# An eighth home for W1 tiles, and a later block 1 whose x is transposed by DMA alone, in the early phase of a two-layer MLP kernel

## The chip, the cores and the metric

The kernel runs on one core of one Trainium2 chip. The time is the device time of one execution in microseconds (us), lower is better. Most executions of one kernel agree within 0.3%.

## The reference

```
x: 16 x 512 x 768, w1: 768 x 3072, b1: 3072, w2: 3072 x 768, all float32
y = x @ w1 + b1
y = 0.5 * y * (1 + erf(y / sqrt(2)))      # gelu
out = y @ w2
```

## The kernel before

The 8192 rows of x are worked off in eight blocks of 1024 rows. Both products use a scheme of the Strassen kind: seven products P1 to P7 of half-size operands in place of eight, at the price of sums of operands (on VectorE, DVE) and of results (DVE and ScalarE, ACT). A *unit* of the first product is one tile of 256 columns of W1 with one block of x. A unit takes seven groups of three matmuls of 512 columns, 4.53 us when nothing waits.

A *W1 tile* in SBUF has seven operands: four raw quarters and three sums that DVE makes (one raw quarter is also replaced by a difference). There are twelve tiles. The first 20 us or so are the *head*: loads, casts, and the first two tiles with block 0 by plain products. In the early phase (blocks 0 and 1) each tile is loaded from W1 by GpSimd's queue (it casts to float16), completed by DVE, used by block 0 and by block 1, and stored once, 672 KB, by SyncE's queue into a scratch in DRAM (`keep`), from where blocks 2 to 7 read it. There are seven *homes* for twelve tiles, so tiles 7 to 11 take over the homes of tiles 0 to 4 when block 1 has used those. The rows of W2 are loaded into the last homes as they come free.

In the code and the profiles, `bX`, `bY`, `bZ` and `bW` are the buffers in PSUM into which TensorE writes the products, `arena` is the memory in SBUF that holds everything else, and c12 and c22 are two of the four quarters of a unit's result. A *slot* is a place between the products of a unit where work for the other engines and queues is emitted. A hole is time in which PE has no matmul to execute.

The order of units and of the loads and stores around them (cut):

```
slots.update({7: slots[0], 8: slots[1], 9: slots[2], 10: slots[3], 11: slots[4]})   # homes of tiles 7 to 11

seq = ([(0, k) for k in range(7)] +                                  # (block, tile)
       [(1, 0), (1, 1), (1, 2), (0, 7), (1, 3), (0, 8), (1, 4), (0, 9), (1, 6), (0, 10), (0, 11),
        (1, 5), (1, 10), (1, 11), (1, 7), (1, 8), (1, 9)])
over = {7: 0, 8: 1, 9: 2, 10: 3, 11: 4}

def loads_a(pos):                      # GpSimd's queue, emitted at slot 5 of unit `pos`
    if pos == 0:
        load_wt(4); load_next_x(1, (0, 4, 1, 5)); load_wt(5)
        load_next_x(1, (2, 6, 3, 7)); load_wt(6)
    for n in range(7, NH):
        if pos == at[1, over[n]] + 1:  # one unit after block 1 used the old tile of that home
            load_wt(n)
    if pos in w2_at_pos:
        load_w2(*w2_at_pos[pos])

X1_PE = (3, 7)                         # x tiles of block 1 that TensorE transposes
def transposes_a(pos):                 # SyncE's queue
    for t in (pos - 1, pos + 3):
        if t not in X1_PE:
            transpose_dma(1, t)

# ... in fill_a(pos, slot), at slot 5:
loads_a(pos)
if pos < 5:
    transposes_a(pos)
for n in {at[1, 0]: (0, 2, 3, 4, 6, 5), at[1, 1]: (1,)}.get(pos, ...):
    keep(n)                            # SyncE's queue too
```

The pipeline of one unit i and of the unit j before it, where the waits below arise (cut): 

```
p1(i); copy_xy(i)   # ACT copies bX into bY once P1 is done
p7(j)               # then DVE adds c22 from bY
fill(1)
p5(i); p3(j)        # then DVE adds c12 from bZ
p6(i)               # into bY; then DVE copies bY into bZ
j.right_done()      # ACT: gelu of c12 and c22
p4(j)               # then ACT: gelu; p2(i), then ACT: gelu
```

Every engine executes its own instructions in this order.

Of the kernel before, what the change touches and what calls it, by code (L numbers as in the profile page):

```python
# [10 lines left out]
P = 128  # L11
ADD = mybir.AluOpType.add
SUB = mybir.AluOpType.subtract
# [4 lines left out]
B11, B21, T1, B22, T3, T2, T4 = range(7)  # L18
# [4 lines left out]
def kernel(  # L23
# [8 lines left out]
    nc = tc.nc  # L32
# [5 lines left out]
    RH = SB // 2  # L38
    nsb = R // SB
    KQ = K // P // 2  # L40
    NH = H // P // 2
# [26 lines left out]
    GR = 4 * NH * RH  # L68
# [20 lines left out]
    def cut(off, n, pattern=None, **dims):  # L89
        ap = arena[:, off:off + n]  # L90
        return ap.rearrange(pattern, **dims) if pattern else ap

    def halves(off):
        return [cut(off + h * (GR // 2), GR // 2, "p (c a r) -> p c a r", c=NH, a=2)
                for h in range(2)]

    Gs = [halves(0), halves(GR)]
# [17 lines left out]
    def wt_at(off):  # L115
        return cut(off, WT_N)

    def w1_raw(wt):
        return wt[:, 0:4 * KQ * P].rearrange("p (k c) -> p k c", c=2 * P)
# [9 lines left out]
    W2P = 2 * W2_N  # L129
    o_far = [o_w2 + W2P, o_w2 + W2P + WT_N, o_w2 + W2P + 2 * WT_N, o_w2 + W2P - WT_N]  # L130
    slots = dict(enumerate([wt_at(o_wt + k * WT_N) for k in range(3)] + [wt_at(o) for o in o_far]))
    slots.update({7: slots[0], 8: slots[1], 9: slots[2], 10: slots[3], 11: slots[4]})
    wt_late = [wt_at(o_wt2), wt_at(o_wt2 + WT_N)] + wt_own[:2]
    wt_far = [wt_at(o_lev + 8 * RH + k * WT_N) for k in range(3)]
    assert 8 * RH + 3 * WT_N <= 8 * LB
# [20 lines left out]
    w2rows = [cut(o_w2 + k * W2P, W2P, "p (c n) -> p c n", c=NH) for k in range(2)]  # L156
# [29 lines left out]
    with tc.manual_schedule():  # L186

        soon, queue, late, slow = [], [], [], []

        def tt(o, a, b, op):  # L190
            nc.vector.tensor_tensor(out=o, in0=a, in1=b, op=op)  # L191

        def later(n, f, q=None):
            (queue if q is None else q).append((70 + n * 0.52, f))
# [8 lines left out]
        def flush(q):  # L203
            while q:
                q.pop(0)[1]()
# [4 lines left out]
        def hi_of(n):  # L210
            sb, k = divmod(n, NH)
            return k if sb < ONE else k // 2 + NQ * (k % 2)

        def load_wt(n):
            hi = hi_of(n)
            if n >= NH:
                sb, k = divmod(n, NH)
                wts[n] = wt_far[k - 4] if 4 <= k < 7 else wt_late[(sb + 2 + k - 7 * (k > 6)) % 4]
                nc.sync.dma_start(out=wts[n], in_=w1s[hi][:])
                return  # L220
            wts[n] = slots[n]
            nc.gpsimd.dma_start(out=w1_raw(wts[n]), in_=w1r[:, :, 2 * hi * P:2 * (hi + 1) * P])

        def keep(n):
            nc.sync.dma_start(out=w1s[hi_of(n)][:], in_=wts[n])

        def prep_wt(n):
            o = {s: w1_op(wts[n], s) for s in range(7)}
            for d, a, b in ((T3, B22, T1), (T1, T1, B11), (T2, B22, T1), (T4, B21, T2)):
                later(KQ * P, lambda d=d, a=a, b=b: tt(o[d], o[a], o[b], SUB), soon)  # L230

        def load_w2(k, c0, c1):
            nc.gpsimd.dma_start(out=w2rows[k][:, c0:c1, :], in_=w2r[:, k, c0:c1, :])
# [65 lines left out]
        def xT_of(sb, t):  # L299
            return XTs[sb][:, t // NU, :, (t % NU) * P:(t % NU + 1) * P]  # L300

        def transpose_dma(sb, t):
            nc.sync.dma_start_transpose(out=xT_of(sb, t), in_=xhs[t])
# [5 lines left out]
        def transpose_pe(sb, t, copy=nc.scalar.copy):  # L309
            for kc in range(2 * KQ):  # L310
                nc.tensor.transpose(out=bT[t % 2][:, kc, :], in_=xhs[t][:, kc * P:(kc + 1) * P],
                                    identity=ident[:])
            copy(out=xT_of(sb, t), in_=bT[t % 2][:])
# [5 lines left out]
        def x_sums(sb, q, r=slice(0, RH), ks=range(4)):  # L319
            A11, A12, A21, A22 = [a[:, :, r] for a in blocks(sb)]  # L320
            S1, S2, S4 = [a[:, :, r] for a in XSs[sb]]
            n = KQ * len(range(RH)[r])
            ops = ((S1, A21, A22, ADD), (S2, S1, A11, SUB), (A21, A11, A21, SUB), (S4, A12, S2, SUB))
            for k in ks:
                later(n, lambda k=k: tt(*ops[k]), q)
# [431 lines left out]
        def plain(n, row, side, half, r=slice(0, RH)):  # L757
            slot = ((B11, T1), (B21, B22))[half][side]
            for c in range(KQ):
                nc.tensor.matmul(out=banks[n, row][side][:, r], lhsT=w1_op(wts[n], slot)[:, c, :],  # L760
                                 rhs=blocks(0)[2 * row + half][:, c, r],
                                 start=half == 0 and c == 0 and r.start == 0,
                                 stop=half == 1 and c == KQ - 1, skip_group_check=True)

        def plain_done(n, row, side):
            nc.scalar.activation(out=Gs[0][side][:, n, row, :], in_=banks[n, row][side][:, 0:RH],
                                 func=GELU, bias=b1t[:, 2 * n + side:2 * n + side + 1])

        top, bottom = slice(0, 2 * P), slice(2 * P, RH)
        for half in range(2):  # L770
            for side in range(2):
                plain(0, 0, side, half)
        for side in range(2):
            plain_done(0, 0, side)
        plain(1, 0, 0, 0)
        transpose_pe(0, 4)
        plain(1, 0, 0, 1)
# [27 lines left out]
        for k in (2, 3):  # L805
            for r in (top, bottom):
# [2 lines left out]
        soon += last  # L809


        seq = ([(0, k) for k in range(7)] +
               [(1, 0), (1, 1), (1, 2), (0, 7), (1, 3), (0, 8), (1, 4), (0, 9), (1, 6), (0, 10), (0, 11),
                (1, 5), (1, 10), (1, 11), (1, 7), (1, 8), (1, 9)])
        at = {u: n for n, u in enumerate(seq)}
        over = {7: 0, 8: 1, 9: 2, 10: 3, 11: 4}

        def load_next_x(sb, ts):
            for t in ts:
# [1 line left out]

        w2_at_pos = {8: (0, 0, 2), 9: (0, 2, 4), 11: (0, 4, 6), 13: (0, 6, 8),
                     at[1, 6] + 1: (0, 8, 10), at[1, 6] + 2: (0, 10, 12),
                     at[1, 5] + 1: (1, 7, 12), at[1, 10] + 1: (1, 0, 3), at[1, 11] + 1: (1, 3, 7)}

        def loads_a(pos):
            if pos == 0:
                load_wt(4)
                load_next_x(1, (0, 4, 1, 5))
                load_wt(5)  # L830
                load_next_x(1, (2, 6, 3, 7))
                load_wt(6)
            for n in range(7, NH):
                if pos == at[1, over[n]] + 1:
                    load_wt(n)
            if pos in w2_at_pos:
                load_w2(*w2_at_pos[pos])

        X1_PE = (3, 7)

        def transposes_a(pos):
            for t in (pos - 1, pos + 3):
                if t not in X1_PE:
                    transpose_dma(1, t)

        def fill_a(pos, slot):
            if pos == 2 and slot == 1:
                plain(1, 1, 1, 1, bottom)
                plain_done(1, 1, 1)
            if pos == at[1, 0] - 2 and slot in (2, 5):  # L850
                transpose_pe(1, X1_PE[slot // 3])
            if slot == (1 if pos < at[1, 0] else 4) and pos + 1 < len(seq) and seq[pos + 1][0] == 0:
                prep_wt(seq[pos + 1][1])
            if slot == 4:
                if pos in (3, 6):
                    prep_wt(pos // 6)
                for m, c in ((21, 9), (22, 0), (23, 3), (23, 6)):
                    if pos == m:
                        prep_w2(T2, c, queue)
                        prep_w2(T3, c, late if m == 23 else queue)  # L860
                if pos == 23:
                    for c in range(0, NH, W2C):
                        prep_w2(T4, c, late)
            if slot == 1:
                if pos in (at[1, 0] - 2, at[1, 0] - 1):
                    h = pos - at[1, 0] + 2
                    x_sums(1, soon, slice(h * RH // 2, (h + 1) * RH // 2))
                if pos == at[0, NH - 1] + 2:
                    for c in range(0, NH, W2C):
                        prep_w2(T1, c, queue)  # L870
                    for k in (0, 1):
                        g_sum(k, 0)
            if pos > at[0, NH - 1]:
                if slot in (1, 4):
                    sums((0, 1100, 0, 0, 1500)[slot])
            elif slot in (1, 2, 4, 5):
                sums((0, 600, 300, 0, 600, 300)[slot])
            if slot == 5:
                loads_a(pos)
                if pos < 5:  # L880
                    transposes_a(pos)
                for n in {at[1, 0]: (0, 2, 3, 4, 6, 5), at[1, 1]: (1,)}.get(
                        pos, seq[pos][1:] if pos > at[1, 6] and seq[pos][0] and seq[pos][1] > 6 else ()):
                    keep(n)
            if slot == 6:
                flush(soon)

# [230 lines left out]
```

## Time and profile before

| | before |
|---|---|
| time, median (three runs) | 853.24 us |
| span of the profiled run | 851.5 us |
| TensorE (PE) busy | 844.9 us, 99% |
| DVE busy | 667.0 us, 78% |

The page of the profile of the kernel before: the span, the busy time of PE with its share and count of instructions, and the chain of work that ended last, by engine (PEld is TensorE's weight load, POOL is GpSimd).

```profile
span 851.5 us, 16488 instructions
PE 844.9 (99%) x6432; PEld 568.8 (67%) x6432; DVE 667.0 (78%) x1128; ACT 420.9 (49%) x686; POOL 83.3 (10%) x135
...
PE 94%; DMA 4%; DVE 1%; ACT 0%; issue 0%; POOL 0%; DVEq 0%; ACTq 0%
```

PE is the limit, so only holes in its stream of matmuls, or work that it need not do, can be won. I find holes by subtracting the start of each matmul from that of the next: 512 columns take 216 ns when nothing waits. The timeline of the kernel before (start, duration, engine, line, operation, output and input, count, and in brackets the idle time before it with what ended it) shows what the early phase holds of both kinds:

```profile
35.44 0.50 PE L311 MATMUL bT<-ident,arena 128*128 128x128 f16 x6
36.37 0.81 ACT L313 COPY arena<-bT 128x768 f16<-128x768 f16 x1
...
37.72 0.50 PE L311 MATMUL bT<-ident,arena 128*128 128x128 f16 x6
...
41.63 1.46 PE L386 MATMUL bY<-arena 128*128 128x512 f16 x6 [0.17 <-ACT bY L604]
...
46.46 0.68 DVE L611 TENSOR_TENSOR arena<-bY,arena 128x512 f32<-128x512 f32 x1
```

The two lines with bT are the PE transposes of two x tiles (they shift the stream by 0.33 us each). At 41.63 us PE waited for ACT's copy into bY (matmul 0.335 us late). The DVE add at 46.46 us released a matmul 0.31 us late; a further hole of 0.08 us is at 45.95 us. Together that is 1.39 us, all that the early phase has to give.

First SyncE's in the timeline: six transposes, issued from 23.35 us on, take it 14.45 us, and then seven stores follow.

```profile
23.35 14.45 SPq L303 DMA_TRANSPOSE arena<-arena  x6
37.89 8.99 SPq L225 DMA_DIRECT2D w1s<-arena  x7
```

GpSimd's load of the first tile that reuses a home (tile 7), in the timeline:

```profile
51.54 0.83 POOL L222 DMA_DIRECT2D arena<-in_w_dram  x1 [26.17 <-PE bZ L386]
```

### The profile page before, as it was taken

Reading aid. Unit: us, or ns where it says so; the run is one execution under the profiler, and the core shown is the slowest. Engines: PE = TensorE matmul, PEld = TensorE weight load, DVE = VectorE, ACT = ScalarE, POOL = GpSimd, SP = SyncE. Lnnn points to the kernel's source line nnn. Section 1 sums busy time; section 2 is a strip of 40 time slices with the busy share of each in tenths; the row PEclk is TensorE's granted clock in tenths of the full one; section 3 lists DMA queues with packets and bytes.
Section 4 is the critical chain, followed back from the end, with each engine's and each line's share of the span. In section 5 each row is a group of like instructions: output and inputs, shape, how many; then the busy total and the mean of one; then the engine's idle time right before and its main releaser. Section 6 shows DMA issues by size and latency. Waiting matters only on the chain.

```text
span 851.5 us, 16488 instructions
## 1 busy us (share of the span) xinstructions
PE 844.9 (99%) x6432; PEld 568.8 (67%) x6432; DVE 667.0 (78%) x1128; ACT 420.9 (49%) x686; POOL 83.3 (10%) x135
## 2 busy tenths in 40 slices
PE   8999999999999999999999999999999999999998
PEld 5444445687544897448974499645995469944798
DVE  4866678786657998579976799668996689956998
ACT  4777762122277512784138722477216771267611
POOL 5021100002100002000020000200002100010000
PEclk9999999999999999999999999999999999999999
DMA  9996986749999599987999689994999969984398
GB/s 227 213 256 89 253 169 244 267 184 221 212 340 226 186 326 372 304 183 233 334 368 292 141 283 335 360 294 113 312 335 355 277 128 325 347 322 172 100 298 295
DMA packets 143522, 219.05 MB, mean 257 GB/s; under 512 B 61756, under 2 KB 84724, under 8 KB 143444
## 3 DMA queue, kind: packets, MB, share of 16 engines
q1 hardware_dynamic: 117968, 179.83, 66.8%
q0 software_dynamic: 25440, 38.15, 20.7%
q8 instruction: 50, 0.82, 0.4%
q14 instruction: 28, 0.23, 0.1%
q10 hardware_dynamic: 36, 0.01, 0.0%
HBM read 180.30 MB, written 47.87 MB: 268 GB/s over the span
## 4 chain that ended last, share of the span: by engine, by line
PE 94%; DMA 4%; DVE 1%; ACT 0%; issue 0%; POOL 0%; DVEq 0%; ACTq 0%
PE bY L386 20%; PE bY L491 15%; PE bX L386 13%; PE bX L491 10%; PE bW L386 7%; PE bZ L386 7%; PE bZ L491 5%; PE bW L491 5%; PE bY L430 5%; DMA arena<-in_x_dram 3%; PE bZ L430 2%; PE bX L430 2%; PE bW L430 2%; DMA arena<-in_w_dram 1%; PE bY L578 1%; DVE arena L191 1%
## 5 line engine op out<-in xcount | busy, mean ns | idle before, releaser
L191 DVE TENSOR_TENSOR arena<-arena 128x1536 f16<-128x1536 f16 (+7 forms) x632 | 402.9, 668 | 7.8 <-DMA arena<-arena 1.6
L386 PEld LDWEIGHTS <-arena 128*128 128x128 f16 x1974 | 192.5, 98 | 224.7 <-issue 1.1
L491 PEld LDWEIGHTS <-arena 128*128 128x128 f16 x3528 | 292.1, 98 | 8.3 <-issue 0.4
L386 PE MATMUL bY<-arena 128*128 128x512 f16 x846 | 214.5, 379 | 0.3 <-ACT bY L604 0.2
L611 DVE TENSOR_TENSOR arena<-bY,arena 128x512 f32<-128x512 f32 (+1 forms) x102 | 69.3, 680 | 126.3 <-PE bY L386 87.6
L491 PE MATMUL bY<-arena 128*128 128x192 f16 x1500 | 138.3, 246 | 0.0
L386 PE MATMUL bX<-arena 128*128 128x512 f16 x564 | 138.2, 379 | 0.0
L604 ACT COPY bY<-bX 128x512 f32<-128x512 f32 (+1 forms) x143 | 78.6, 550 | 119.3 <-DVE arena L540 81.9
L402 ACT ACTIVATE arena<-arena,b1t 128x1024 f16<-128x1024 f32 x94 | 108.0, 1149 | 54.4 <-DVE arena L639 54.4
L624 ACT COPY arena<-bW 128x512 f32<-128x512 f32 (+1 forms) x147 | 81.0, 551 | 91.0 <-PE bW L491 43.9
L491 PE MATMUL bX<-arena 128*128 128x192 f16 x1020 | 93.1, 246 | 0.1
L639 DVE TENSOR_TENSOR arena<-bZ,arena 128x512 f32<-128x512 f32 (+1 forms) x102 | 69.2, 679 | 20.7 <-PE bZ L386 17.9
L386 PE MATMUL bZ<-arena 128*128 128x512 f16 x282 | 76.2, 379 | 0.0
L386 PE MATMUL bW<-arena 128*128 128x512 f16 x282 | 76.2, 379 | 0.0
L430 PEld LDWEIGHTS <-arena 128*128 128x128 f16 x528 | 51.6, 98 | 34.1 <-issue 0.2
L523 POOL DMA_DIRECT2D out_dram<-arena x42 | 30.5, 728 | 404.8 <-DVE arena L635 368.2
L407 ACT ACTIVATE arena<-bX,b1t 128x512 f16<-128x512 f32 x94 | 64.0, 681 | 10.0 <-PE bX L386 10.0
L407 ACT ACTIVATE arena<-bY,b1t 128x512 f16<-128x512 f32 x94 | 63.3, 673 | 0.0
L655 ACT COPY bZ<-bY 128x512 f32<-128x512 f32 (+1 forms) x54 | 29.0, 537 | 65.9 <-DVE arena L639 33.7
L297 POOL DMA_DIRECT2D arena<-in_x_dram x60 | 32.3, 544 | 250.8 <-DMA arena<-arena 141.3
L491 PE MATMUL bZ<-arena 128*128 128x192 f16 x504 | 48.5, 246 | 0.0
L491 PE MATMUL bW<-arena 128*128 128x192 f16 x504 | 48.5, 246 | 0.0
(60 smaller groups left out, 398.9 us busy)
## 6 DMA issues: line engine op xcount, KB each, us to landing
arena<-w2s SPq DMA_DIRECT2D x294, 288.0 KB, 4.6
arena<-w1s SPq DMA_DIRECT2D x72, 672.0 KB, 7.1
out_dram<-arena POOLq DMA_DIRECT2D x42, 384.0 KB, 7.2
w2s<-arena SPq DMA_DIRECT2D x49, 288.0 KB, 3.7
arena<-in_x_dram POOLq DMA_DIRECT2D x60, 192.0 KB, 7.3
w1s<-arena SPq DMA_DIRECT2D x12, 672.0 KB, 6.6
arena<-in_w_dram POOLq DMA_DIRECT2D x17, 384.0 KB, 7.4
out_dram<-arena SPq DMA_DIRECT2D x17, 384.0 KB, 3.3
```

Source lines behind the costliest of these rows:

```text
L191: nc.vector.tensor_tensor(out=o, in0=a, in1=b, op=op)
L297: nc.gpsimd.dma_start(out=xhs[t], in_=xr[:, sb * 8 + t, :])
L386: nc.tensor.matmul(out=dst[:, 0:RH], lhsT=w1_op(self.wt, slot)[:, c, :], rhs=a[:, c, :], start=first and c == 0, stop=c == self.C - 1, ski ...
L402: nc.scalar.activation(out=self.G[1][:, hi, :, :], in_=self.tmp, func=GELU, bias=b1t[:, 2 * hi + 1:2 * hi + 2])
L407: nc.scalar.activation(out=self.G[0][:, hi, row, :], in_=bank[:, 0:RH], func=GELU, bias=b1t[:, 2 * hi:2 * hi + 1])
L430: nc.tensor.matmul(out=dst[:, 0:N2], lhsT=a, rhs=w[:, :, c, :], start=first and c == 0, stop=c == self.C - 1, skip_group_check=True)
L491: nc.tensor.matmul(out=dst[:, t * N4:(t + 1) * N4], lhsT=a, rhs=w[:, c, :], start=first and c == 0 and t == ts[0], stop=c == NQ - 1, skip_ ...
L523: eng.dma_start(out=orr[:, s0:s0 + 2, right * N2:(right + 1) * N2], in_=self.dst[:, r].rearrange("p t h n -> p t (h n)"))
L604: nc.scalar.copy(out=bY[u.g % 2][:, 0:u.F], in_=bX[u.g % 2][:, 0:u.F])
L611: nc.vector.tensor_tensor(out=u.c22(), in0=bY[u.g % 2][:, 0:u.F], in1=w[:, 0:u.F], op=ADD)
L624: nc.scalar.copy(out=w[:, 0:u.F], in_=bW[:, 0:u.F])
L639: nc.vector.tensor_tensor(out=u.c12(), in0=bZ[:, 0:u.F], in1=w[:, 0:u.F], op=ADD)
```

## The change

The intent: take the two PE transposes off TensorE by giving them to the DMA engines; to give these time, begin block 1 one unit later, which takes one more tile of W1 and so an eighth home (in a part of block 1's output that is written late); and relieve DVE at 38 to 47 us by making six sums of tiles 0 and 1 in the head, where DVE idles, and by spreading the sums of block 1's x. The first load of W2 rows, which would otherwise be free to start at once, is held back by a dummy copy. The diff, cut to its core:

```
-    slots.update({7: slots[0], 8: slots[1], 9: slots[2], 10: slots[3], 11: slots[4]})
+    slots.update({7: wt_at(GR + 8 * 2 * RH), 8: slots[0], 9: slots[1], 10: slots[2], 11: slots[3]})
...
+        prep_wt(0, range(3))            # head: three of four sums of tile 0; later the same for tile 1
+        flush(soon)
...
-        seq = ([(0, k) for k in range(7)] +
-               [(1, 0), (1, 1), (1, 2), (0, 7), (1, 3), (0, 8), (1, 4), (0, 9), (1, 6), (0, 10), (0, 11),
-                (1, 5), (1, 10), (1, 11), (1, 7), (1, 8), (1, 9)])
+        seq = ([(0, k) for k in range(8)] +
+               [(1, 0), (1, 1), (1, 2), (0, 8), (1, 3), (0, 9), (1, 4), (0, 10), (1, 6), (0, 11),
+                (1, 5), (1, 11), (1, 7), (1, 10), (1, 8), (1, 9)])
-        over = {7: 0, 8: 1, 9: 2, 10: 3, 11: 4}
+        over = {8: 0, 9: 1, 10: 2, 11: 3}
...
-                     at[1, 5] + 1: (1, 7, 12), at[1, 10] + 1: (1, 0, 3), at[1, 11] + 1: (1, 3, 7)}
+                     at[1, 5] + 1: (1, 4, 12), at[1, 11] + 1: (1, 0, 4)}
...
-                load_wt(6)
+                for n in (6, 7):
+                    load_wt(n)
...
+            if pos == at[1, 0]:
+                nc.gpsimd.tensor_copy(out=w2rows[0][:, 0, 0:1], in_=Gs[0][0][:, 5, 1, 0:1])
...
-        X1_PE = (3, 7)
...
-                if t not in X1_PE:
-                    transpose_dma(1, t)
+                transpose_dma(1, t)
...
-                    x_sums(1, soon, slice(h * RH // 2, (h + 1) * RH // 2))
+                        x_sums(1, soon, slice(h * RH // 2, (h + 1) * RH // 2), (0, 1))
+                if pos == at[1, 0]:
+                    x_sums(1, soon, ks=(2, 3))
...
-                for n in {at[1, 0]: (0, 2, 3, 4, 6, 5), at[1, 1]: (1,)}.get(
-                        pos, seq[pos][1:] if pos > at[1, 6] and seq[pos][0] and seq[pos][1] > 6 else ()):
+                for n in range(7) if pos == at[0, 7] else seq[pos][1:] if pos > at[0, 7] and not seq[pos][0] else ():
                     keep(n)
+                if pos == at[0, 7] + 1:
+                    keep(7)
```

More of the change, by code (lines that the diff above doesn't have):

```diff
@@ L225, in keep, with prep_wt @@
             nc.sync.dma_start(out=w1s[hi_of(n)][:], in_=wts[n])
-        def prep_wt(n):
+        def prep_wt(n, ks=()):
             o = {s: w1_op(wts[n], s) for s in range(7)}
-            for d, a, b in ((T3, B22, T1), (T1, T1, B11), (T2, B22, T1), (T4, B21, T2)):
-                later(KQ * P, lambda d=d, a=a, b=b: tt(o[d], o[a], o[b], SUB), soon)
+            early = ((T3, B22, T1, SUB), (T2, T3, B11, ADD), (T4, B21, T2, SUB), (T1, T1, B11, SUB))
+            usual = ((T3, B22, T1, SUB), (T1, T1, B11, SUB), (T2, B22, T1, SUB), (T4, B21, T2, SUB))
+            for d, a, b, op in [early[k] for k in ks] if ks else usual:
+                later(KQ * P, lambda d=d, a=a, b=b, op=op: tt(o[d], o[a], o[b], op), soon)
         def load_w2(k, c0, c1):
@@ L774 @@
             plain_done(0, 0, side)
+        prep_wt(1, range(3))
+        flush(soon)
         plain(1, 0, 0, 0)
@@ L831, in loads_a @@
                 load_next_x(1, (2, 6, 3, 7))
-                load_wt(6)
-            for n in range(7, NH):
+                for n in (6, 7):
+                    load_wt(n)
+            for n in range(8, NH):
                 if pos == at[1, over[n]] + 1:
                     load_wt(n)
+            if pos == at[1, 0]:
+                nc.gpsimd.tensor_copy(out=w2rows[0][:, 0, 0:1], in_=Gs[0][0][:, 5, 1, 0:1])
             if pos in w2_at_pos:
                 load_w2(*w2_at_pos[pos])
-        X1_PE = (3, 7)
         def transposes_a(pos):
             for t in (pos - 1, pos + 3):
-                if t not in X1_PE:
-                    transpose_dma(1, t)
+                transpose_dma(1, t)
         def fill_a(pos, slot):
@@ L849, in fill_a @@
                 plain_done(1, 1, 1)
-            if pos == at[1, 0] - 2 and slot in (2, 5):
-                transpose_pe(1, X1_PE[slot // 3])
             if slot == (1 if pos < at[1, 0] else 4) and pos + 1 < len(seq) and seq[pos + 1][0] == 0:
@@ L854, in fill_a @@
             if slot == 4:
-                if pos in (3, 6):
-                    prep_wt(pos // 6)
+                if pos in (3, 4):
+                    prep_wt(pos - 3, (3,))
                 for m, c in ((21, 9), (22, 0), (23, 3), (23, 6)):
@@ L864, in fill_a @@
             if slot == 1:
-                if pos in (at[1, 0] - 2, at[1, 0] - 1):
-                    h = pos - at[1, 0] + 2
-                    x_sums(1, soon, slice(h * RH // 2, (h + 1) * RH // 2))
+                for h in range(2):
+                    if pos == at[1, 0] - 2 + h:
+                        x_sums(1, soon, slice(h * RH // 2, (h + 1) * RH // 2), (0, 1))
+                if pos == at[1, 0]:
+                    x_sums(1, soon, ks=(2, 3))
                 if pos == at[0, NH - 1] + 2:
```

## The prediction

> **What bounds the kernel now.** TensorE. The page gives PE 844.9 us busy of an 851.5 us span (99%), granted clock 1.00; the chain of waits is 94% PE. A change that leaves the matmuls alone can win only gaps between them. The trace's matmul start times show, after the first 10 us (a head whose length this change leaves alone), only these gaps: 41.08 us (0.335 us too long; the wait view names the ACT copy into bY), 45.95 us (0.08), 46.67 us (0.31, released by the DVE add into c22), 387 us (0.25, not touched). Add the two PE transposes of block 1's x at 35.44 and 37.72 us: six 128-column matmuls each, 0.33 us, 0.67 us in all. The stake is about 1.39 us, 0.16% of 853.24.
>
> **Removed.** The two PE transposes and their ACT copies from PSUM (0.80 us each). Six of the eight DVE sums of W1 tiles 0 and 1 (0.35 us each) go to the head, where DVE idles (4.25 us before 14.91 us, timeline). That, and spreading block 1's x sums (0.55 us per 128x768) over three units, lowers DVE from 5.7 us of work per 4.53 us unit at 38 to 47 us to about 4.6. The 0.31 and 0.08 us gaps should vanish.
>
> **Added, moved.** Two more DMA transposes (SyncE spends about 1.3 us issuing one). Tile 7's load (384 KB, 2 us at the software queue's 200 KB/us) moves from 51.5 to about 25.5 us. The Trainium skill, "DMA: Bandwidth & Descriptors", section "Issuing engines are not separate DMA queues", says that all issuers share 16 DMA engines and interleave. The trace agrees: the software queue moves 198 KB/us alone at 20 us, 120 to 130 at 31 to 33 us beside the transposes. So I estimate from those rates that tile 7 lands at 39 to 40 us and the last transpose at about 44 us (before: 40.75). Both are needed just then: tile 7 by DVE at about 40, the transposes by the x sums at about 44.5. The late W2 load of eight row chunks (1.5 MB written, 8 us) should land near 111.5 us, about 1 us after DVE wants it, with about as much slack before PE notices.
>
> **On the critical path.** The 0.67 us surely; the 0.39 us of DVE-caused gaps almost surely. The 0.335 us gap is a chain: tile 6 lands at 36.28 us, DVE waits 0.55 us for it, its sums delay the c12 add, ACT's gelus follow late, the copy into bY is late. Without transposes PE asks 0.67 us earlier and tile 6 lands no earlier: 0.2 to 0.3 us of it stays. New waits for tile 7 or the last transposes: 0.1 to 0.2 us expected, up to 1 us if they land a us later. Net gain about 0.95 us.
>
> **Predicted time: 852.3 us, 8 in 10 within 851.4 to 853.3.** Faster by over 2%: 0.005; within 2%: 0.99; slower by over 2%: 0.005.
>
> **Right if:** no PE transposes after 30 us; no DVE-released gap near 46 us; a small ACT-released gap left near 40.5 us; a span of about 850.5 us, with the difference made before 50 us and everything after 55 us merely shifted.
>
> **Wrong if:** the last DMA transposes land after 45 us and DVE, which executes in order, waits in them before the c12 add; tile 7 delays tile 6; or the 1.5 MB W2 transfer lands after 113 us and PE waits near 115 us. Then the gain is eaten and the time stays at 853.

## More of the kernel before

The queue of SyncE carries, in order, the DMA transposes of block 1's x and then the stores of the W1 tiles.

```profile
arena<-in_w_dram POOLq DMA_DIRECT2D x1, 384.0 KB, 5.0
```

Tile 7's load landed 5.0 us after its issue, at 56.58 us. The last store landed at 52.79 us, so the two hardly met.

## The result, and the profile after

| | before | after |
|---|---|---|
| time, median of six runs | 853.30 us | 858.17 us |
| lowest and highest | 853.23, 853.92 | 857.74, 859.07 |
| ratio, 95% interval | | 1.0057 (1.0044 to 1.0070) |
| span of the profiled run | 851.5 us | 857.3 us |

A ratio here and below is the mean time of a kernel's runs over that of the kernel before in the same rounds, so it is not quite the ratio of the medians. The change made the kernel 4.9 us slower; it lies well outside the predicted range. The profiled run of the changed kernel is its slowest of six (859.07).

The page of the changed kernel (its line numbers are those of before plus two, so L386 is now L388):

```profile
span 857.3 us, 16467 instructions
PE 846.1 (99%) x6420; PEld 568.5 (66%) x6420; DVE 667.0 (78%) x1126; ACT 419.9 (49%) x684; POOL 83.0 (10%) x135
...
PE 92%; DMA 3%; issue 3%; DVE 0%; SPq 0%; POOL 0%; POOLq 0%
```

Twelve matmuls fewer (the transposes), and yet a longer span, while PE is "99% busy" in both: the busy share says little here. What says where the time went is the start of the same group of matmuls (P5, into bW) in each unit, read from both traces:

```
unit        2      9      10     11     12     22      23
before    22.49  54.31  58.84  63.38  67.91  113.23  117.77
after     23.35  53.99  58.52  67.68  72.72  118.04  123.31
after-before +0.86 -0.32 -0.32  +4.30  +4.81   +4.81   +5.54
```

There are four pieces. The head (before unit 2) was 0.86 us longer in this one run; of the ten other runs below with the same head only `hold_one` shows it (unit 2 at 23.18 us; the rest at 21.94 to 22.48). Then units 2 to 9 gained 1.18 us, as intended. Unit 11 lost 4.6 and unit 12 another 0.5 us. Unit 23 lost 0.7 us.

**Unit 11.** The timeline of the changed kernel, GpSimd, PE and DVE at that place (lines of other engines left out):

```profile
55.74 0.85 POOL L222 DMA_DIRECT2D arena<-in_w_dram  x1 [9.79 <-PE bZ L388]
...
61.11 0.81 PE L388 MATMUL bX<-arena 128*128 128x512 f16 x3
65.17 1.54 DVE L191 TENSOR_TENSOR arena<-arena 128x384 f16<-128x384 f16 x4 [3.66 <-DMA arena<-in_w_dram]
65.19 1.42 PE L388 MATMUL bX<-arena 128*128 128x512 f16 x3 [3.27 <-DMA arena<-in_w_dram]
66.40 1.49 PE L388 MATMUL bY<-arena 128*128 128x512 f16 x3
...
67.68 1.31 PE L388 MATMUL bW<-arena 128*128 128x512 f16 x3
```

PE waits 3.27 us for a tile of W1, tile 8, which was issued at 55.74 us, and whose time to landing the DMA view of that one issue gives:

```profile
arena<-in_w_dram POOLq DMA_DIRECT2D x1, 384.0 KB, 9.4
```

That is 9.4 us where the like load before took 5.0. The issue itself is no later with respect to the unit that uses the tile (two units ahead in both kernels). After the wait three matmuls take 1.28 us instead of 0.65. The windows view says why (stretch, its length, busy us of PE, PEld, DVE, ACT and POOL with counts, then granted TensorE clock, DMA share and GB/s):

```profile
61.50:65.00 3.50, 0.42 (x2) 0.00 (x0) 0.01 (x1) 1.54 (x3) 0.00 (x0) 1.00 1.28 223
65.20:68.80 3.60, 3.60 (x9) 1.32 (x10) 2.10 (x5) 0.57 (x1) 0.00 (x0) 0.53 1.31 244
```

After the idle stretch the granted clock was 0.53 in the mean of these 3.6 us (0.50 from 65.28 to 68.69 us). By the starts of the matmuls the wait cost 3.44 us and the slow clock another 1.69 us. The Trainium skill, "TensorE: Matmul & The Clock Gate", section "Why this matters for your kernels", advises no gaps over about 3 us of idle PE; this trace agrees, with 3.27 us of idle and 1.69 us of penalty. (`hold_one` below lost the clock after 2.0 us.)

**What held up tile 8.** SyncE's queue in the timeline after:

```profile
23.75 20.75 SPq L305 DMA_TRANSPOSE arena<-arena  x8
44.59 7.85 SPq L225 DMA_DIRECT2D w1s<-arena  x8
```

Eight transposes kept SyncE for 20.75 us instead of 14.45 (six), about 2.5 us for each instead of the 1.3 us that the prediction reckoned with, so the stores behind them began at 44.59 instead of 37.89 us, eight instead of seven. Their last landed at 63.41 instead of 52.79 us. The DMA view of the stretch 53 to 61 us (packets, bytes and share of the 16 engines, by queue; q1 is the queue of SyncE's transfers, q0 that of GpSimd's):

```profile
DMA packets 715, 3.38 MB, mean 422 GB/s; under 512 B 85, under 2 KB 87, under 8 KB 715
...
q1 hardware_dynamic: 708, 3.38, 101.8%
q0 software_dynamic: 7, 0.00, 0.2%
```

While the stores ran at 422 GB/s, GpSimd's queue, in which tile 8 had stood since 55.74 us, moved nothing.

**Unit 23.** The wait views of 100 to 125 us after (engine and line, what it waited for, us in total, times, longest), one of DVE and one of PE:

```profile
DVE arena L191 <- DMA arena<-in_w_dram: 2.5, 2, 2.1
```

```profile
PE bY L388 <- DVE arena L613: 0.6, 1, 0.6
```

DVE waited 2.1 us for W2 rows, and with it the add of c22 that PE needs. The DMA view of that load: one transfer of eight chunks, 11.1 us to landing.

```profile
arena<-in_w_dram POOLq DMA_DIRECT2D x1, 1536.0 KB, 11.1
```

### The profile page after: what moved, and what is told of

Same layout as the page of the kernel before. It is cut to its first block, busy times and chain, and to the rows that moved or that the text cites. A ratio compares the mean times of both kernels' runs of the same rounds, so it can differ in the third digit from the quotient of the medians. Undisturbed runs are those within 1.5% of the kernel's fastest.

```text
span 857.3 us, 16467 instructions
## 1 busy us (share of the span) xinstructions
PE 846.1 (99%) x6420; PEld 568.5 (66%) x6420; DVE 667.0 (78%) x1126; ACT 419.9 (49%) x684; POOL 83.0 (10%) x135
## 4 chain that ended last, share of the span: by engine, by line
PE 92%; DMA 3%; issue 3%; DVE 0%; SPq 0%; POOL 0%; POOLq 0%
PE bY L388 19%; PE bY L493 14%; PE bX L388 13%; PE bX L493 10%; PE bW L388 6%; PE bZ L388 6%; PE bZ L493 5%; PE bW L493 5%; PE bY L432 5%; DMA arena<-in_w_dram 3%; PE bW L432 2%; PE bX L432 2%; PE bZ L432 2%; PE bY L580 1%; PE bX L580 1%
## 5 line engine op out<-in xcount | busy, mean ns | idle before, releaser
L191 DVE TENSOR_TENSOR arena<-arena 128x768 f16<-128x768 f16 (+4 forms) x630 | 403.3, 671 | 12.2 <-DMA arena<-in_w_dram 6.2
L388 PEld LDWEIGHTS <-arena 128*128 128x128 f16 x1974 | 193.0, 98 | 230.0 <-DMA arena<-in_w_dram 3.8
L388 PE MATMUL bY<-arena 128*128 128x512 f16 x846 | 215.2, 380 | 0.6 <-DVE arena L613 0.6
L388 PE MATMUL bX<-arena 128*128 128x512 f16 x564 | 139.0, 380 | 3.3 <-DMA arena<-in_w_dram 3.3
L388 PE MATMUL bW<-arena 128*128 128x512 f16 x282 | 76.7, 381 | 0.0
L388 PE MATMUL bZ<-arena 128*128 128x512 f16 x282 | 76.2, 379 | 0.0
```

The costliest lines, as they stand in the source:

```text
L191: nc.vector.tensor_tensor(out=o, in0=a, in1=b, op=op)
L388: nc.tensor.matmul(out=dst[:, 0:RH], lhsT=w1_op(self.wt, slot)[:, c, :], rhs=a[:, c, :], start=first and c == 0, stop=c == self.C - 1, ski ...
```

## The experiments

Theory A: the stores are a backlog. They start late (because of the transposes in front) and are one more, and tile 8's load does not get through until they are drained. Theory B: GpSimd's queue itself is slow, or full of the W2 load that stands before tile 8; the stores have nothing to do with it. `hold_keeps`, `late_w2`, `pe_tr` and `split_w2` shared a chip and the runs of the kernel before (median 853.19).

### hold_keeps: half of the stores later

```
-  for n in range(7) if pos == at[0, 7] else ...: keep(n)
-  if pos == at[0, 7] + 1: keep(7)
+  for n in {at[0, 7]: (0, 1, 2, 3), at[0, 8]: (8,), at[0, 9]: (9, 4, 5),
+            at[0, 10]: (10, 6, 7), at[0, 11]: (11,)}.get(pos, ()): keep(n)
```

> The changed kernel, but the stores of W1 tiles 4, 5, 6, 7 wait behind those of tiles 9 and 10 (only 0 to 3 are stored at once). Theory A (backlog of stores: eight stores of 672 KB start at 44.6 us because SyncE is busy issuing transposes until then, and tile 8's load, issued at 55.7 us, gets no DMA share before they drain at about 61 us): the four stores end near 53 us, tile 8 lands by 60 us, the 3.4 us PE wait at 61.5 us and the half-speed matmuls after it vanish, total about 853.0 us (852.6 to 853.6), with the 0.7 us wait near 119 us left. Theory B (the W2 load at 45.3 us and tile 8 sit in one software queue and that queue is slow): stores do not matter, time stays at 857.5 to 858.5.

Measured: 852.79 us (852.33 to 853.39), ratio 0.9996 (0.9980 to 1.0013): 5.4 us less than the changed kernel, at the speed of the kernel before. Tile 8's load, with the same place in the order of units (issued at 54.61 us), landed 5.2 us after its issue (the DMA view of that issue):

```profile
arena<-in_w_dram POOLq DMA_DIRECT2D x1, 384.0 KB, 5.2
```

In the wait view of PE from 40 to 130 us the wait for W1 is gone; only the W2 one is left:

```profile
PE bY L388 <- DVE arena L613: 0.2, 1, 0.2
```

Theory A holds in its main point: with four of the eight stores moved behind it, tile 8 lands as fast as in the kernel before. B, that the stores have nothing to do with it, is refuted.

### late_w2: no W2 load before unit 11

```
-  w2_at_pos = {8: (0, 0, 2), 9: (0, 2, 4), 11: (0, 4, 6), 13: (0, 6, 8),
+  w2_at_pos = {11: (0, 0, 4), 13: (0, 4, 8),        # and the dummy copy removed
```

> The changed kernel, but no W2 rows are loaded before unit 11 (two loads of four row chunks instead of four of two; the hold copy on GpSimd falls away). Theory B (W2 loads ahead in the software queue delay tile 8): tile 8 lands near 61 us as its queue is empty, the wait vanishes, about 853 us. Theory A (store backlog): the stores lose only the 2 us that the first W2 load took, tile 8 lands at about 63 us instead of 65.15, PE still waits about 1.3 us, total about 855.5 us (854.8 to 856.5).

Measured: 853.93 us (853.64 to 854.32), 1.0009 (0.9994 to 1.0023). PE still waits for tile 8, but 1.3 us, and the clock stays up:

```profile
PE bX L388 <- DMA arena<-in_w_dram: 1.3, 1, 1.3
PE bY L388 <- DVE arena L613: 0.4, 1, 0.4
```

Both theories missed the number. The wait shrank by 2.0 us as A said, but I had left out that the 1.69 us of slow clock go with it. So the W2 load is a part of the backlog, not a rival to it: its bytes stand before the last six stores, and these before tile 8.

### pe_tr: the two PE transposes back, the rest as changed

```
+  X1_PE = (3, 7)           # transpose_dma only for the others
+  if pos == at[1, 0] - 2 and slot in (2, 5): transpose_pe(1, X1_PE[slot // 3])
```

> The changed kernel, but x tiles 3 and 7 of block 1 go through PE again (two DMA transposes fewer, as before the change). Theory A: SyncE reaches the first store about 3 to 4.5 us earlier (40 to 41.5 us), the eight stores end near 59.5 us, tile 8 lands near 61.5 us, the wait shrinks to under 1 us and with it the slow clock, PE pays 0.67 us for the transposes: about 854.3 us (853.5 to 855.5). Theory B (software queue alone): 858.8 us, as the transposes only add 0.67 us.

Measured: 853.51 us (853.34 to 854.10), 1.0005 (0.9990 to 1.0019). SyncE's first store is issued at 39.36 us, tile 8 lands 6.6 us after its issue, and the wait is 0.5 us:

```profile
39.36 8.17 SPq L225 DMA_DIRECT2D w1s<-arena  x8
```

```profile
PE bY L388 <- DVE arena L613: 0.9, 1, 0.9
PE bX L388 <- DMA arena<-in_w_dram: 0.5, 1, 0.5
```

(The first fence is SyncE's line of the timeline, the second the wait view of PE from 40 to 130 us.) Two DMA transposes are enough to move the stores by 5.2 us (0.9 of it is the later head of the changed kernel's run). The eighth home and the eighth store remain in this kernel, and it still waits a little: each part adds to one backlog.

### hold_one: the store of tile 7 alone later

```
-  if pos == at[0, 7] + 1: keep(7)
+  if pos == at[0, 9]: keep(7)       # behind tile 9's store
```

> The changed kernel with the store of tile 7 alone held back (behind tile 9's store), so seven stores stand before tile 8's load, as many as in the kernel before. Backlog theory: one store of 672 KB takes 1.6 us, so tile 8 lands about 1.6 us earlier (63.5 instead of 65.15), PE's wait falls from 3.4 to about 1.6 us, and since waits of 1.5 us and less left the clock alone the 1.6 us of half-speed matmuls vanish too: about 854.9 us (854.3 to 855.6). Rival (the stores as such do not matter, only the total in the early phase or the W2 load): no change, about 858.

Measured: 855.47 us (854.67 to 857.25), 1.0021 (1.0005 to 1.0038), on another chip than those four. The wait fell by 1.23 us by matmul starts, against the 1.6 expected:

```profile
PE bX L388 <- DMA arena<-in_w_dram: 2.0, 1, 2.0
PE bY L388 <- DVE arena L613: 0.2, 1, 0.2
```

The half of the expectation about the clock failed in the profiled run, which was the slowest of the four: after 2.0 us of idle PE the clock dropped, as the windows view shows (columns as above):

```profile
60.22:63.63 3.41, 1.37 (x8) 0.44 (x6) 0.88 (x3) 2.30 (x3) 0.53 (x1) 1.00 1.20 169
63.63:67.05 3.42, 3.42 (x9) 1.22 (x10) 1.99 (x5) 0.57 (x1) 0.00 (x0) 0.50 1.18 240
```

It seems to have held in the other three executions: their mean granted clock was 1.000 (this one's 0.998), and they took 854.67 to 855.62 us. Whether the clock falls differs from execution to execution of one kernel: in `w2_gate` two executions at 1.000 took 856.21 and 856.56 us, two at 0.998 took 857.78 and 858.25.

### w2_gate: the first small W2 load issued after all stores

```
-  nc.gpsimd.tensor_copy(out=w2rows[0][:, 0, 0:1], in_=Gs[0][0][:, 5, 1, 0:1])
+  nc.gpsimd.tensor_copy(out=w2rows[0][:, 0, 0:1], in_=Gs[0][0][:, 7, 1, 0:1])
```

> The changed kernel with the first small W2 load (two row chunks, 384 KB) released by a later unit's gelu, at about 53 us instead of 45 us, when all eight stores have been issued. If the DMA engines serve the two queues in the order of issue, this load lands only after the last store, that is at about 61 us (8 us after its issue), the stores end at about 59 us, and tile 8, behind it, still lands at about 64 to 65 us: about 857.5 us. If they interleave the queues packet by packet, the load lands at about 57 to 58 us and the stores end about 2 us later.

Measured: 857.17 us (856.21 to 858.25), 1.0045 (1.0030 to 1.0060). The W2 load, issued at 53.94 us, landed at 61.86 us, after the last store (59.97 us). The DMA view of that issue, and then that of 54 to 59 us:

```profile
arena<-in_w_dram POOLq DMA_DIRECT2D x1, 384.0 KB, 7.9
```

```profile
q1 hardware_dynamic: 359, 1.75, 103.2%
q0 software_dynamic: 2, 0.00, 0.4%
```

So for stores and loads the engines did not interleave: what was issued later from the other queue came later. In the changed kernel, where this load was issued at 45.26 us between the second and the third store, its packets did run in between (at 49 to 52 us), and the stores all but stopped meanwhile (0.03 MB of theirs and 0.33 MB of its own from 50 to 52 us). Here PE waited 2.6 us for tile 8 (61.75 to 64.35 us) and the clock stayed at 1.00:

```profile
59.05:62.46 3.41, 2.70 (x13) 1.02 (x11) 1.65 (x3) 2.48 (x4) 0.85 (x1) 1.00 1.16 181
62.46:65.87 3.41, 1.52 (x8) 0.70 (x9) 1.43 (x4) 0.98 (x2) 0.00 (x0) 1.00 1.29 203
65.87:69.28 3.41, 3.41 (x17) 1.56 (x16) 2.08 (x3) 1.99 (x3) 1.51 (x2) 1.00 1.16 287
```

The stretches are not chosen freely. In the clock records of all 14 profiles the clock changes only at whole multiples of 3.413 us after its first rise (in the changed kernel the rise is at 3.84 us, the fall 18 of them later at 65.28, the recovery 19 later at 68.69), and each fall in mid-kernel lasted one such interval. Counted by interval, PE sat idle for 3.27 us (changed kernel), 2.75 (`split_w2`) and 2.04 (`hold_one`) before a fall, and for 1.89 at most where none came: the wait here lies across a boundary, 0.71 us on one side and 1.89 on the other. The ends of the kernels, where PE falls idle, agree: 2.13 us of idle in one interval brought a fall in `late_w2`, 1.84 us none in `split_w2`.

PE also lost 1.09 us at 48.6 us in this run, where DVE waited 1.4 us for the last transposes, as it does in `fixed_w6` below.

### split_w2: the late W2 load in two

```
-  at[1, 5] + 1: (1, 4, 12), at[1, 11] + 1: (1, 0, 4)}
+  at[1, 5] + 1: (1, 7, 12), at[1, 11] + 1: (1, 0, 4), at[1, 7] + 1: (1, 4, 7)}
```

> The changed kernel, but the late W2 load of chunks 4 to 11 is split: 7 to 11 at the same point, 4 to 6 two units later. If the 0.74 us PE gap near 119.8 us comes from DVE waiting for the whole eight-chunk transfer (landed 118.62 us), chunks 7 to 11 land about 3 us earlier and the gap vanishes: 0.7 us less than the changed kernel, about 857.4 us. The rival (that gap comes from lateness left over from the stall at 61 us, or from the stores of W2 that share the DMA) leaves it at 858.1 us.

Measured: 857.85 us (855.79 to 859.36), 1.0053 (1.0036 to 1.0069). The time alone proves nothing, its spread is wider than the effect (the fastest execution had a mean clock of 1.000, the slowest 0.995). The profile does: the five chunks landed 7.8 us after their issue, and in the wait view of PE from 40 to 130 us the wait for DVE is gone, the one for tile 8 not.

```profile
arena<-in_w_dram POOLq DMA_DIRECT2D x1, 960.0 KB, 7.8
```

```profile
PE bX L388 <- DMA arena<-in_w_dram: 2.8, 1, 2.8
```

### head_only and dma_tr_only: single parts in the kernel before

`head_only` has the six sums in the head and nothing else of the change. `dma_tr_only` has `X1_PE = ()` and nothing else.

> The kernel before with one part of the change alone: six of the eight DVE sums of W1 tiles 0 and 1 in the head. My theory: DVE is then no longer overloaded at 38 to 47 us, the gaps of 0.08 and 0.31 us near 46 us vanish, the 0.34 us gap at 41 us stays: about 852.8 us against 853.2. A rival says that the sums in the head delay the head itself (the changed kernel's profile had its head 0.86 us later): then 853.5 to 854.

Measured: 852.98 us (852.54 to 853.77), 0.9995 (0.9979 to 1.0010) against 853.18: nothing that stands out of the spread. Its head was the earliest of all profiles (unit 2's P5 at 21.88 us), so the sums don't delay the head; the 0.86 us of the changed kernel's profile were that run's. But the holes did not vanish, they moved; the wait view of PE from 30 to 125 us:

```profile
PE bY L388 <- ACT bY L606: 0.6, 1, 0.6
PE bY L388 <- DVE bZ L659: 0.2, 1, 0.2
```

PE, being earlier in this run, waited longer for a chain that starts at tile 6's landing. My expectation that the DVE holes go with this part alone is not borne out.

> The kernel before with one part of the change alone: all eight x tiles of block 1 by DMA transposes, no PE transposes, the sequence of units as before. Without the eighth home block 1 begins at about 42.5 us and its x sums want the last transposes at about 38 to 40 us, but they land at about 43.5 us: DVE and PE wait 2 to 4 us, and the stores begin 3 us later, which also delays tile 7's load: about 856 us (854.5 to 858). The rival, that DMA transposes are free, gives 853.2 less 0.67, about 852.5 us.

Measured: 854.75 us (854.57 to 855.05), 1.0016 (1.0002 to 1.0029): without the later block 1 the DMA transposes cost 1.6 us, less than I expected, with PE waiting behind DVE:

```profile
PE bY L386 <- DVE bZ L657: 2.3, 2, 1.7
```

DMA transposes are not free here; in the runs below, with the eighth home and its later block 1, there is room for them.

### fixed: both repairs

hold_keeps and split_w2 in one kernel, five rounds.

> Both repairs together: stores of W1 tiles 4 to 7 held back as in hold_keeps, and the late W2 load split as in split_w2. If the two losses are separate (store backlog before tile 8; one large W2 transfer), PE waits neither near 61 us nor near 115 us, and the time is hold_keeps less its 0.41 us gap: about 852.4 us (852.0 to 852.9), 0.8 us below the kernel before. If the second gap is fed by the held-back stores, it stays and the time is 852.8.

Measured: 852.55 us (852.19 to 853.37) against 853.18, ratio 0.9990 (0.9978 to 1.0003). The interval still includes 1, so this gain is not clear of noise. The wait view of PE from 30 to 125 us is empty; holes of 0.25, 0.08, 0.14 and 0.08 us between matmuls remain at 38 to 50 us, as the separate-losses view expected.

### fixed_w6: tile 6 loaded earlier

```
-  load_next_x(1, (2, 6, 3, 7)); load_wt(6); load_wt(7)
+  load_next_x(1, (2, 6)); load_wt(6); load_next_x(1, (3, 7)); load_wt(7)
```

> As fixed, and tile 6 of W1 is loaded before x tiles 3 and 7 of block 1 instead of after them. If the 0.35 us gap near 38 us (PE on the ACT copy into bY) comes from tile 6 landing at 35.9 us, through DVE's sums and ACT's gelu, tile 6 now lands about 2 us earlier (near 34 us) and the gap vanishes: 0.35 us below fixed, about 852.05 us. Rival: ACT itself is the limit there, or the x tiles come too late for their transposes; then the time is that of fixed or more.

Measured: 853.53 us (852.86 to 853.57), 0.9999 (0.9986 to 1.0011): 1 us worse than fixed, the rival's outcome. The hole at 38 us went, as the theory said, but a larger one (1.32 us) came at 47.5 us. The wait views of PE and of DVE from 30 to 60 us:

```profile
PE bY L388 <- DVE bZ L659: 1.2, 1, 1.2
```

```profile
DVE arena L191 <- DMA arena<-arena: 1.6, 1, 1.6
```

DVE waits 1.6 us for the last transpose in the sums of x, and the c12 add and the copy into bZ, which PE needs sooner, stand behind those sums.

### fixed_w6_s4 and fixed_s4: those sums behind the add

```
   if slot == 1:
-      for h in range(2):
-          if pos == at[1, 0] - 2 + h:
-              x_sums(1, soon, slice(h * RH // 2, (h + 1) * RH // 2), (0, 1))
+      if pos == at[1, 0] - 2:
+          x_sums(1, soon, slice(0, RH // 2), (0, 1))
   if slot == 4:
+      if pos == at[1, 0] - 1:
+          x_sums(1, soon, slice(RH // 2, RH), (0, 1))
```

> As fixed_w6, and the second half of block 1's x sums is put on DVE after the c12 add and the copy into bZ of that unit, not before them. In fixed_w6 PE waited 1.3 us at 47.5 us; if that is DVE, which executes in order, waiting 1.6 us in those sums for the last DMA transpose (landed 46.36 us) with the c12 add behind them, the wait vanishes though the transposes land no earlier: 853.5 less 1.3, about 852.2 us. Rival: the first sum itself is needed by PE (P5 of block 1's first unit at about 48.5 us) and the wait only moves: 853 or more.

Measured: 851.92 us (851.86 to 852.30, six runs) against 853.30, ratio 0.9985 (0.9971 to 0.9998). Between the head and 125 us no hole over 0.04 us is left in the stream of matmuls. DVE no longer waits for a transpose in those sums (the last one landed at 45.45 us in this run, 0.9 us earlier than in fixed_w6, so the new place of the sums is not the only difference). The page:

```profile
span 850.1 us, 16469 instructions
PE 844.7 (99%) x6420; PEld 568.7 (67%) x6420; DVE 667.2 (78%) x1126; ACT 419.8 (49%) x684; POOL 84.0 (10%) x136
```

> As fixed (tile 6 loaded after all x tiles), with the same later place of the second half of the x sums. Gaps of fixed that it can remove: 0.14 us at 47.4 and 0.08 at 49.4; the 0.25 us gap at 38 us (tile 6) stays: about 852.3 us, 0.2 below fixed, and 0.1 above fixed_w6_s4 if tile 6's wait is real.

Measured: 852.48 us (852.22 to 852.62), 0.9989 (0.9975 to 1.0003). Only the hole of tile 6 is left (0.44 us and 0.08 after it). The difference from fixed_w6_s4, 0.56 us, is what loading tile 6 earlier is worth once nothing stands behind the transposes. That is more than the 0.1 us I expected.

## Why the prediction was right or wrong

- **Right: the stake, and that it can be collected.** The prediction put it at 1.39 us. fixed_w6_s4, which has no new wait left, is 1.38 us faster than before (853.30 to 851.92). The changed kernel's units 2 to 9 gained 1.18 us, but that is in part luck: with its late head PE came to tile 6 and to the last transposes late enough. `split_w2`, whose code is the same to that point, had a head of 22.02 us and gained only 0.30 us there, and `w2_gate` (22.22 us) 0.23.
- **Right: no PE transposes, no DVE-released hole near 46 us.** 0.2 us of new holes came near 48 and 50 us; that is the size expected for "new waits for tile 7 or the last transposes". The chain from tile 6 over DVE and ACT, predicted to leave 0.2 to 0.3 us, is seen in fixed (0.25), hold_keeps (0.35), fixed_s4 (0.44) and split_w2 (0.77), which all have unit 2 at 22.03 us or earlier, and not in the changed kernel's own profile (23.35), whose late head hid it.
- **Wrong: "the difference made before 50 us and everything after 55 us merely shifted".** This step failed. I followed the transposes to the sums of x that need them, and not to what stands behind them in SyncE's queue. The prediction allowed about 1.3 us of SyncE for each of the two more transposes; they took 6.3 us in all (20.75 less 14.45), and the trace of before already showed 14.45 us for six. The stores began 6.7 us later (in part because of that run's late head; in hold_keeps, with an early head, 5.2 us) and were one more, and tile 8's load met them: 3.44 us of wait and 1.69 us of slow clock. hold_keeps, which moves only stores, gives it all back; hold_one, late_w2 and pe_tr each give back a part.
- **Wrong: that the two queues interleave.** The prediction cited the Trainium skill, "DMA: Bandwidth & Descriptors", section "Issuing engines are not separate DMA queues", and found it in the trace for loads beside transposes. For loads behind stores it did not hold: nothing for GpSimd's queue at 53 to 61 us (0.00 of 3.38 MB), and in w2_gate none either. With fair shares tile 8 should have come sooner (reckoned, not tested). I took what one pair of transfers showed for all.
- **Mis-sized: the last transpose.** Estimated at about 44 us, it landed at 46.03 in the changed kernel's run, 44.90 in hold_keeps and 46.36 in fixed_w6. That cost little in the changed kernel, 1.1 us in w2_gate and 1.3 us in fixed_w6.
- **Mis-sized: the large W2 load.** Estimated to land at 111.5 us, about 1 us late with as much slack. It landed at 118.62 us, which is 113.8 without the 4.8 us that the kernel was late by then. It took 11.1 us to landing where the prediction reckoned 8 us for its bytes; DVE waited 2.1 us and PE lost 0.74 us. The danger was named in the prediction, but given no weight in the sum.
- **The sum.** Losses by matmul starts: 3.44 + 1.69 + 0.74 = 5.87; gain 1.18; net 4.69. With the 0.86 us of the late head that is the 5.5 us between the two profiles; the medians differ by 4.87.

What stays open: why loads and stores were served in the order of issue when loads and transposes took turns. That a wait of 2.6 us left the clock alone (w2_gate) and one of 2.0 us did not (hold_one) fits the intervals of 3.413 us shown under w2_gate; no run moved a wait within its interval to test that.

## What to carry to other kernels

When work is moved onto a queue, follow what stands behind it in that queue, to the end of its backlog, and ask which load that backlog will meet; the work moved may itself arrive in time. Work without a deadline, such as stores for a later phase, should be queued behind transfers that have one. Put an instruction that may have to wait for a DMA behind the instructions of the same engine that others wait for: these moves, with the split of one large load and an earlier load of one tile, turned a loss of 4.9 us into a gain of 1.4.

## What the Trainium skill lacked or had wrong

- "DMA: Bandwidth & Descriptors", section "Issuing engines are not separate DMA queues", says that transfers from different issuers interleave. Here a 384 KB load from GpSimd's queue made no progress behind stores of 672 KB issued earlier by SyncE: 0.00 of 3.38 MB in 53 to 61 us, 9.4 us to landing instead of 5.0; issued after eight stores in w2_gate it landed after the last of them. Beside DMA transposes the same queue did get on (120 to 130 KB/us), and the packets of the two queues took turns: 699 of GpSimd's and 702 of SyncE's from 31 to 34 us in the kernel before.
- "TensorE: Matmul & The Clock Gate", section "Why this matters for your kernels", puts the limit at about 3 us of idle PE. The clock halved for 3.41 us after waits of 3.3, 2.8 and 2.0 us, and did not after waits of 2.6 and 1.3 us: waits well under 3 us can already cost it. The same page's section "What's actually happening" describes an observation window of 3413 ns that runs free of the kernel, and the traces agree: the clock changed at multiples of 3.413 us alone, with a phase of its own in each execution. But the window need not be wholly idle: 2.04 us of idle in one was enough, 1.89 us was not.
- No page tells how long issuing DMA transposes holds SyncE on this chip while other transfers run; "DMA: Bandwidth & Descriptors" has only cycles of the sequencer per instruction, for "previous generations" beside those of trn3. Here eight of 192 KB kept its queue for 20.75 us beside a busy GpSimd queue, six kept it 14.45 us, and everything behind them waited.
